# Ranking experts by token count and running them in strips of 128, 64 or 32 slots

## The chip, the cores and the metric

One Trainium2 chip, one of its cores. The metric is device time of one execution in microseconds (us), the median of several runs. TensorE (PE) has two clock levels, 1.2 and 2.4 GHz; the profile gives the granted share of the higher one. All times here come from one profiled execution, its trace, or the three timed runs.

## The reference

Two networks follow each other on a sequence of 256 tokens, width 1024. The first has two layers, each an attention and spatial-gating mixer, then a mixture of experts (MoE). The second is an attention block with an MLP and a recurrent (rwkv) block with an MLP, beside a context stream of its own. The change is in the MoE:

```python
# per layer, T = 256 tokens, D = 1024, 64 experts, top 8 of them for each token
scores = sigmoid(xt @ router_w)
eidx   = top_k(masked(scores + router_bias), 8)     # 4 of 8 groups of experts survive first
wts    = scores[eidx] / sum(scores[eidx]) * 2.5
routed = sum over the 8 experts e of a token:  wts[e] * ((silu(x @ w_gate[e]) * (x @ w_up[e])) @ w_down[e])
out    = routed + (silu(xt @ ws_gate) * (xt @ ws_up)) @ ws_down
```

`w_gate[e]` and `w_up[e]` are 1024 x 256, `w_down[e]` is 256 x 1024, all float32: 3.15 MB for an expert, 201.3 MB for a layer. 256 x 8 = 2048 pairs of a token and an expert fall on 64 experts, 32 on the average. With the inputs of the reference the fullest experts of layer 0 get 109, 99, 73, 56, 55 tokens, those of layer 1 get 75, 73, 71, 67, 63; from the 33rd on by rank no expert has more than 27 and 30.

## The kernel before

`moe` runs twice. It computes the router (lines 507 to 556), gives every pair of token and expert its place in the expert's list (`pos`, 558 to 568), and works in **groups of 256 slots**. A group is 4 experts with 64 slots each; an expert with more than 64 tokens sends the rest to a "wild" block of 64 slots. There are 16 groups of fixed experts and one of 4 wild blocks, 17 in all. Should there be more wild blocks than 4, `overflow` runs a loop; with the inputs here there are 3 and 4.

A group is two **pairs**, each of 128 slots, so that two experts fill the 128 partitions of a PSUM tile. Its steps, all on PE through `mm` (line 75):

- `pick`: a one-hot matrix `oh` (VectorE) gathers the tokens of the 256 slots, 32 products of 128 x 256 into `gat`; ScalarE and VectorE move them to `xe`.
- `up`: for each pair, 8 slices of the width times 2 experts, products with 64 columns of `xe` as weights and 512 columns of gate and up weights streaming, into `gu`. An expert uses one half of the array's columns. Each product in float32 is two records in the trace.
- `down`: silu and product (`hs`, `hm`), two transposes (`hp`), then products with `w_down` into `yps`; ScalarE and VectorE scale by the slot's weight `wsl` and split the result into `yH` and `yL`.
- `scatter`: 16 products with the transposed one-hot `ohT` into `sca`; VectorE adds them to the result.

Expert weights are fetched by SP (`fetch`, line 625) into tiles of 1 MB from a pool of 7 (`we`): 2 tiles for gate and up of an expert (two DMAs of 512 KB each), 1 for down. The address is a constant. The wild blocks' weights are gathered by POOL with an index (`wild_weights`).

Between the groups the second network's context stream runs as **side work**: `side_work(BG_GROUP / 2)` is called twice in a group and emits steps until their nominal cost (the number that each yields) is 7.25 us, so 14.5 a group. In layer 0 it is attention and an MLP, with weights of their own, in layer 1 the rwkv context. The rest of it runs later beside the second network (`late_path`).

The framework's scheduler sets the final order on each engine. PE and SP then run in that order: a PE instruction that waits for weights holds all behind it, and an SP transfer that waits for a free tile holds all transfers behind it.

Of the kernel before, what the change touches and what calls it, by code (L numbers as in the profile page):

```python
# [13 lines left out]
F32 = mybir.dt.float32  # L14
F32R = mybir.dt.float32r
I32 = mybir.dt.int32
# [11 lines left out]
NWILD = 4  # L28
NBLK = NE + NWILD
SLOT = 64  # L30
MAXOVER = 32
WU = 2048
WP = 1024
BG_MIX = 4
BG_GROUP = 14.5
# [6 lines left out]
class Net:  # L42
# [55 lines left out]
    def wtile(self, shape, srcs, name="w"):  # L98
        v = self.wbuf(shape, name)
        for sl, src in srcs:  # L100
            self.nc.sync.dma_start(v if sl is None else v[(slice(None),) + sl], src)
        return v

    def setup(self):
# [10 lines left out]
        self.identR = c.tile([P, P], F32R, name="identR")  # L115
        nc.vector.tensor_copy(self.identR, self.ident)
        self.ios = c.tile([P, SLOT], F32, name="ios")
        nc.gpsimd.iota(self.ios, pattern=[[1, SLOT]], base=0, channel_multiplier=0,
# [10 lines left out]
        self.slotp = c.tile([P, 1], F32, name="slotp")  # L129
        nc.vector.tensor_copy(self.slotp[:64], pf[:64])  # L130
        nc.vector.tensor_scalar_add(self.slotp[64:], pf[64:], -64.0)
        names = ["c", "c_2", "c_ctx_2"]
        st = c.tile([24, P], F32, name="cst0")
# [5 lines left out]
        nc.scalar.activation(cc, ps, AF.Silu)  # L139
        self.lhs1 = c.tile([P, KT, 32], F32, name="lhs1")  # L140
# [360 lines left out]
    def moe(self, l, x, row, mc, mce, rw, rb):  # L501
# [44 lines left out]
        mask = pp.tile([P, 2, NE], F32, name="mask")  # L546
        nc.vector.tensor_scalar(mask, mr, 3.0e38, None, op0=OP.is_equal)
        self.wt = mp.tile([P, 2, NBLK], F32, name="wt")
        wt = self.wt[:, :, :NE]
        nc.vector.tensor_tensor(wt, sc, mask, op=OP.mult)  # L550
        wsum = pp.tile([P, 2], F32, name="wsum")
        nc.vector.reduce_sum(wsum, wt, axis=AX.X)
        wrec = pp.tile([P, 2], F32, name="wrec")
        nc.vector.reciprocal(wrec, wsum)
        for t in range(2):
            nc.vector.tensor_scalar(wt[:, t, :], wt[:, t, :], wrec[:, t:t + 1], 2.5, op0=OP.mult, op1=OP.mult)
# [5 lines left out]
        cn = self.tr([NE, P], "cn")  # L562
        for t in range(2):
            self.mm(cn, mask[:, t, :], self.ones, t == 0, t == 1)
        self.pos = mp.tile([P, 2, NBLK], F32, name="pos")
        pm = self.pos[:, :, :NE]
        nc.vector.scalar_tensor_tensor(pm, rk, 1000.0, mask, op0=OP.add, op1=OP.mult)
        nc.vector.tensor_scalar_add(pm, pm, -1000.0)
        nb = pp.tile([NE, P], F32, name="nb")
        nb1 = pp.tile([NE, P], F32, name="nb1")  # L570
        nc.vector.tensor_scalar(nb, cn, 64.0, None, op0=OP.is_gt)
        for th in (128.0, 192.0):
            nc.vector.tensor_scalar(nb1, cn, th, None, op0=OP.is_gt)
            nc.vector.tensor_tensor(nb, nb, nb1, op=OP.add)
# [7 lines left out]
                                       op0=OP.mult, op1=OP.add)  # L582
        nover = mp.tile([1, 1], I32, name="nover")
        nc.vector.tensor_copy(nover, self.se[0:1, 1, NE - 1:NE])
        idx = mp.tile([P, NWILD], I32, name="idx")
        self.wild(l, self.iow[:, 0:NWILD], NWILD, self.pos[:, :, NE:], self.wt[:, :, NE:], idx, pp)

# [29 lines left out]
        with tc.If(rv > NWILD):  # L617
            self.overflow(l, mce)
# [3 lines left out]
        posT, wHL = self.tables(self.pos, self.wt, NBLK, mp)  # L622
        nq = NBLK // 4

        def fetch(q, pr):
            if q == NE // 4:
                return self.wild_weights(l, [idx[:, 2 * pr + u:2 * pr + u + 1] for u in range(2)])
            b = 4 * q + 2 * pr
            gus = [[self.wtile([2, 4, 256], [((v,), dap(i[n], (l * NE + b + u) * D * 256 + 1024 * a,
                                                        [[KT * 256, P], [256, 4], [1, 256]]))  # L630
                                             for v, n in enumerate(("w_gate", "w_up"))], "gu")
                    for u in range(2)] for a in range(2)]
# [90 lines left out]
    def pick(self, pos, b0, wHL, mce, wk):  # L723
# [36 lines left out]
        for h in range(2):  # L760
            nc.vector.reduce_sum(wsl[64 * h:64 * h + 64, :], wps[64 * h:64 * h + 64, :, h, :], axis=AX.X)
# [1091 lines left out]
```

## Time and profile before

| | us |
|---|---|
| median of 3 runs (lowest, highest) | 3387.86 (3383.33, 3391.14) |
| the profiled execution | 3384.59 |
| its span | 3382.8 |
| mean granted clock | 0.928 |

| engine | busy us | share of the span |
|---|---|---|
| PE | 3123.4 | 92% |
| VectorE (DVE) | 1866.9 | 55% |
| ScalarE (ACT) | 1244.5 | 37% |
| POOL | 484.9 | 14% |

The two MoE layers' groups fill 331 to 1165 us and 1471 to 2222 us, 1585 us together. PE is busy there nearly all the time, and the 16 DMA engines for 0.87 and 0.83 of it. Matmuls are pipelined, so a record is longer than the step from one to the next; rates are read from starts.

### The profile page before, as it was taken

What the parts mean: (1) busy time and instruction counts of PE and PEld (TensorE: products, weight loads), DVE (VectorE), ACT (ScalarE), POOL (GpSimd) and SP (SyncE); (2) the same over time, 40 slices, a digit from 0 to 9 for tenths busy, and PEclk for the clock granted to TensorE, in tenths of its full rate; (3) what the DMA queues carried; (4) which work ended last, traced back from release to release, by engine and by line L of the source; (5) the groups of instructions that cost most, each with busy time, mean ns of one, the idle gap of its engine ahead of it and who ended that gap; (6) DMA issues with size and microseconds to landing.
All of it is one profiled execution on the core that took longest, in us unless ns stands there. A gap on an engine that the chain in (4) does not pass through costs nothing.

```text
span 3382.8 us, 51453 instructions
## 1 busy us (share of the span) xinstructions
PE 3123.4 (92%) x20494; PEld 2095.9 (62%) x20494; DVE 1866.9 (55%) x3553; ACT 1244.5 (37%) x2170; POOL 484.9 (14%) x675
## 2 busy tenths in 40 slices
PE   6998999999999999999999999879999897889899
PEld 2776444554555687765455455556588786777698
DVE  3666444333344675753354345487777757475477
ACT  2563334232223356421232232245444453332343
POOL 1111000000000100110000100213023205243022
PEclk9999999999999999999999999979999895566799
DMA  9764987989988876478888887634425440001352
GB/s 346 276 220 147 374 321 297 349 343 348 336 306 314 307 249 231 173 276 297 331 317 312 332 329 297 254 111 164 151 93 170 132 131 7 10 8 63 146 187 88
DMA packets 240852, 773.33 MB, mean 229 GB/s; under 512 B 24672, under 2 KB 39944, under 8 KB 208864
## 3 DMA queue, kind: packets, MB, share of 16 engines
q1 hardware_dynamic: 230896, 728.56, 59.0%
q0 software_dynamic: 9376, 40.35, 3.3%
q8 instruction: 165, 2.70, 0.3%
q10 hardware_dynamic: 336, 1.06, 0.1%
q14 instruction: 79, 0.65, 0.1%
HBM read 763.73 MB, written 6.18 MB: 228 GB/s over the span
## 4 chain that ended last, share of the span: by engine, by line
PE 43%; DVE 9%; ACT 2%; issue 1%; DMA 0%; POOL 0%; DVEq 0%; SPq 0%; ACTq 0%; POOLq 0%
PE gu L75 7%; PE mu L75 5%; PE w L75 4%; PE yps L75 3%; PE rk L75 2%; PE zy L75 2%; PE gat L75 2%; PE sca L75 2%; PE rv L75 1%; PE rsc L75 1%; PE r L75 1%; PE sa L75 1%; PE aq L75 1%; DVE wl L232 1%; DVE MT L1488 1%
## 5 line engine op out<-in xcount | busy, mean ns | idle before, releaser
L232 DVE TENSOR_TENSOR wl<-w,wh 128x1024 fp32r<-128x1024 f32 (+1 forms) x432 | 467.2, 1087 | 295.1 <-ACT wh L231 289.6
L231 ACT CAST wh<-w 128x1024 fp32r<-128x1024 f32 (+1 forms) x432 | 378.3, 882 | 490.3 <-PE mu L75 135.8
L75 PE MATMUL gu<-gu,xe 128*64 128x512 f32 x2048 | 535.5, 600 | 0.2 <-DMA gu<-in_w_up_dram 0.2
L75 PEld LDWEIGHTS gu<-gu,xe 128*64 128x64 f32 x2048 | 154.2, 137 | 272.4 <-issue 254.8
L75 PE MATMUL yps<-dn,hTe 128*64 128x512 f32 x1024 | 269.8, 611 | 2.4 <-ACT hTe L797 1.6
L807 DVE SCALAR_TENSOR_TENSOR yL<-yps,wsl,yH 128x512 fp32r<-128x512 f32 x136 | 101.7, 750 | 222.4 <-ACT yH L806 222.0
L75 PE MATMUL mu<-hTH,wh 128*128 128x256 f32 x768 | 218.8, 289 | 2.9 <-ACT wh L231 1.6
L75 PE MATMUL mu<-hTL,wh 128*128 128x256 f32 x768 | 217.0, 286 | 0.0
L75 PE MATMUL mu<-hTH,wl 128*128 128x256 f32 x768 | 210.4, 288 | 1.9 <-DVE wl L232 1.9
L784 DVE TENSOR_TENSOR hm<-hs,gu 128x256 f32<-128x256 f32 x68 | 41.5, 610 | 255.8 <-ACT hs L782 255.8
L806 ACT ACTIVATE yH<-yps,wsl 128x512 fp32r<-128x512 f32 x136 | 93.5, 688 | 220.2 <-PE yps L75 213.8
L75 PEld LDWEIGHTS yps<-dn,hTe 128*64 128x64 f32 x1024 | 85.7, 139 | 135.3 <-issue 123.9
L75 PEld LDWEIGHTS mu<-hTH,wh 128*128 128x128 f32 x768 | 149.1, 194 | 12.8 <-issue 4.9
L75 PE MATMUL w<-wl,aTH 128*128 128x512 f32 x384 | 152.8, 398 | 4.4 <-DVE wl L232 4.3
L75 PEld LDWEIGHTS mu<-hTL,wh 128*128 128x128 f32 x768 | 148.9, 194 | 4.0 <-issue 2.5
L75 PE MATMUL w<-wh,aTL 128*128 128x512 f32 x384 | 150.6, 393 | 0.5 <-DVE aTL L232 0.5
L75 PEld LDWEIGHTS mu<-hTH,wl 128*128 128x128 f32 x768 | 144.4, 194 | 10.4 <-issue 4.8
L75 PEld LDWEIGHTS gat<-oh,xL 128*128 128x128 f32 x544 | 103.5, 190 | 75.9 <-issue 57.9
L782 ACT ACTIVATE hs<-gu 128x256 f32<-128x256 f32 x68 | 26.1, 383 | 331.2 <-PE gu L75 330.9
L75 PE MATMUL adaps<-adaw,lhs 128*32 128x512 f32 x768 | 122.9, 653 | 26.5 <-DMA adaw<-in_w_ada_dram 20.5
L75 PE MATMUL gat<-oh,xL 128*128 128x256 f32 x544 | 144.7, 301 | 1.1 <-DVE oh L729 1.1
L75 PE MATMUL w<-wh,aTH 128*128 128x512 f32 x384 | 138.3, 398 | 4.1 <-DVE y L1114 2.6
(601 smaller groups left out, 6669.5 us busy)
## 6 DMA issues: line engine op xcount, KB each, us to landing
gu<-in_w_gate_dram SPq DMA_DIRECT2D x256, 512.0 KB
gu<-in_w_up_dram SPq DMA_DIRECT2D x256, 512.0 KB
dn<-in_w_down_dram SPq DMA_DIRECT2D x128, 1024.0 KB
w<-in_mlp_w_dram SPq DMA_DIRECT2D x96, 1024.0 KB
adaw<-in_w_ada_dram SPq DMA_DIRECT2D x48, 1024.0 KB
adaw<-in_ada_w_dram SPq DMA_DIRECT2D x48, 1024.0 KB
w<-in_w_in_dram SPq DMA_DIRECT2D x30, 1024.0 KB
w<-in_rwkv_w_rkv_dram SPq DMA_DIRECT2D x20, 1024.0 KB
```

Source lines behind the costliest of these rows:

```text
L75: return self.nc.tensor.matmul(out, lhsT, rhs, start=start, stop=stop, skip_group_check=True)
L231: self.nc.scalar.copy(h, f)
L232: self.nc.vector.tensor_tensor(l, f, h, op=OP.subtract)
L782: nc.scalar.activation(hs, gu[:, :256], AF.Silu)
L784: nc.vector.tensor_tensor(hm.rearrange("q j p -> q p j"), hs.rearrange("q (p j) -> q p j", j=2), gu[:, 256:].rearrange("q (p j) -> q p j", ...
L806: nc.scalar.activation(yH[:, sl], y, AF.Copy, scale=g["wsl"][:, p_:p_ + 1])
L807: nc.vector.scalar_tensor_tensor(yL[:, sl], y, g["wsl"][:, p_:p_ + 1], yH[:, sl], op0=OP.mult, op1=OP.subtract)
L1488: nc.vector.transpose(T[r, :, c].rearrange("s n t -> s t n"), FA[p, w].rearrange("n s t -> n t s"))
```

## The change

The 64 experts are ranked on chip by their token count. The 4 fullest get 128 slots each, the next 28 get 64, the last 32 get 32. That is 2 groups of two 128-slot experts, 7 of four 64-slot experts and 4 of eight 32-slot experts: 13 groups of 256 slots, in the order given by `ORDER`. The wild group is gone; `overflow` would run if any expert had more tokens than its slots, which the counts above do not reach. Weights are fetched by rank, so the addresses come from a list of experts `ei` that SP reads into registers. The side work of a group depends on its strip: 0, 12 or 40 us nominal, 244 for a layer against 246.5.

```diff
+CAPS = ((4, 128), (28, 64), (32, 32))
+GROUP = 256
+ORDER = (128, 64, 32, 64, 64, 32, 64, 32, 64, 64, 32, 64, 128)
-BG_GROUP = 14.5
+BG_GROUP = {128: 0, 64: 12, 32: 40}
...
+        cn = self.tr([P, P + NE], "cn")
+        for h in range(2):
+            for t in range(2):
+                self.mm(cn[64 * h:64 * h + 64, :P], mask[:, t, :], self.ones, t == 0, t == 1)
+        for t in range(2):
+            self.mm(cn[:, P:], self.ones, mask[:, t, :], t == 0, t == 1)
...
+        nc.vector.scalar_tensor_tensor(kc, cn[:, 0:1], 64.0, self.slotp[64], op0=OP.mult, op1=OP.subtract)
+        nc.vector.scalar_tensor_tensor(kr, cn[:, P:], 64.0, self.ioe, op0=OP.mult, op1=OP.subtract)
+        nc.vector.tensor_scalar(kr, kr, kc, None, op0=OP.is_gt)
+        nc.vector.reduce_sum(rank, kr, axis=AX.X)
+        for h in range(2):
+            r = slice(64 * h, 64 * h + 64)
+            nc.vector.tensor_scalar(pm2[r, h], self.ioe[r], rank[r], None, op0=OP.is_equal)
+        self.mm(eps, ebc, pm2[:NE, 0], True, True)
+        nc.vector.tensor_copy(self.ei, eps[0:1])
...
+        for t in range(2):
+            self.transpose(mps[:, t, :], mw[:, t].rearrange("p a b -> p (a b)"))
+        nc.scalar.copy(mwT, mps)
+        for t in range(2):
+            self.mm(mso[:, t].rearrange("p a b -> p (a b)"), mwT[:, t, :], pm2.rearrange("p a b -> p (a b)"), True, True)
+        nc.vector.tensor_copy(mask, mso[:, :, 0])
+        nc.scalar.copy(self.wt, mso[:, :, 1])
...
-        self.wild(l, self.iow[:, 0:NWILD], NWILD, self.pos[:, :, NE:], self.wt[:, :, NE:], idx, pp)
...
-        with tc.If(rv > NWILD):
+        with tc.If(rv > 0):
             self.overflow(l, mce)
...
+            r0, w = groups[q]
+            k = P // w
+            with tc.issue_after(behind.pop(0)) if len(behind) > 1 else ExitStack():
+                rvs = [nc.values_load(self.ei[0:1, r0 + pr * k + u:r0 + pr * k + u + 1],
+                                      engines=[mybir.EngineType.SP], min_val=0, max_val=NE - 1) for u in range(k)]
+            src = lambda n, u, j: i[n][l, bass.DynSlice(rvs[u], 1)].rearrange("e (p j) f -> p (e j) f", j=j)
...
         for j in range(KT):
             for v in range(2 if wild else 1):
-                for u in range(2):
+                for u in range(k):
...
-                        self.mm(gu[64 * u:64 * u + 64, :].rearrange("p (a b) -> p a b", a=2), sx(j, u),
+                        self.mm(gu[w * u:w * u + w, :].rearrange("p (a b) -> p a b", a=2), sx(j, u),
                                 gus[j // 4][u][:, :, j % 4, :], j == 0, j == KT - 1)
...
-                for u in range(2):
-                    self.mm(y[64 * u:64 * u + 64, :], hT[:, j, 64 * u:64 * u + 64], dn[u][:, j, sl], j == 0, j == 1)
+                for u in range(P // w):
+                    self.mm(y[w * u:w * u + w, :], hT[:, j, w * u:w * u + w], dn[u][:, j, sl], j == 0, j == 1)
```

The bytes of a transfer and its rows of 4 KB stay as they are. Three places of the built programs show what moves.

SP, fetching expert weights in layer 0 (`gu` tiles are gate and up, `dn` is down). Before:

```order
L101 DMA gu_2805<-in_w_gate_dram 128x1024
L101 DMA gu_2805<-in_w_up_dram 128x1024
L101 DMA dn_2808<-in_w_down_dram 128x2048
L101 DMA dn_2810<-in_w_down_dram 128x2048
L101 DMA gu_2841<-in_w_gate_dram 128x1024
L101 DMA gu_2841<-in_w_up_dram 128x1024
```

After, at the first 32-slot group:

```order
L102 ISA
L102 DMA gu_3440<-in_w_gate_dram 128x1024
L102 ISA
L102 DMA gu_3440<-in_w_up_dram 128x1024
L689 TENSOR_LOAD ei_2428
L689 ISA x2
```

An address computation stands ahead of every transfer, and each fetch is preceded, two fetches early, by one register load for each expert (three more follow the one shown).

PE, the first 64-slot group that is in its stride, layer 0 (`adaps`, `asps`, `atp` are side work). Before:

```order
L75 MATMUL gu<-gu,xe 64x512 x9
L75 MATMUL adaps<-adaw,lhs_100 32x512 x4
L75 MATMUL asps<-kT,qT 128x256
L75 MATMUL adaps<-adaw,lhs_100 32x512 x4
L75 MATMUL asps<-kT,qT 128x256
L75 MATMUL gu<-gu,xe 64x512 x7
L79 MATMUL atp<-ident,ap 128x128 x4
L79 MATMUL hp<-ident,hm 128x128 x2
L75 MATMUL asps<-kT,qT 128x256 x2
L75 MATMUL gu<-gu,xe 64x512
L75 MATMUL yps<-dn,hTe 64x512 x8
```

After, the first 32-slot group:

```order
L76 MATMUL gu<-gu,xe 32x512 x17
L80 MATMUL atp<-ident,ap 128x128 x4
L76 MATMUL asps<-kT,qT 128x256 x2
L80 MATMUL atp<-ident,ap 128x128 x4
L76 MATMUL aops<-apT,v 64x256 x4
L76 MATMUL adaps<-adaw,lhs_117 32x512 x8
L76 MATMUL gu<-gu,xe 32x512
L76 MATMUL asps<-kT,qT 128x256
L76 MATMUL gu<-gu,xe 32x512
L76 MATMUL asps<-kT,qT 128x256
L76 MATMUL gu<-gu,xe 32x512 x13
```

A pair's products come in runs of 16 instead of 8, each of which needs four 1 MB tiles at once instead of two, with more side work between the runs.

PE, from the router's last use to the shared expert (`shp`, `shd`), layer 0. Before:

```order
L75 MATMUL shp<-hT,w 128x256 x22
L75 MATMUL rk<-mask,triS 128x64
L75 MATMUL rk<-mask,ones 128x64
L75 MATMUL rk<-mask,triS 128x64
L75 MATMUL cn<-ones,mask 64x128 x2
L75 MATMUL shp<-hT,w 128x256 x4
L79 MATMUL aps<-ident,araw 128x128 x4
L75 MATMUL adaps<-adaw,lhs_100 32x512 x8
L75 MATMUL sps<-triS,nb 128x64
L75 MATMUL sps<-triI,nb 128x64
L75 MATMUL shd<-w,sT 128x512 x8
```

After:

```order
L76 MATMUL shp<-hT,w 128x256 x22
L76 MATMUL cn<-ones,mw 64x128 x4
L76 MATMUL cn<-mw,ones 128x64 x2
L76 MATMUL shp<-hT,w 128x256 x4
L80 MATMUL aps<-ident,araw 128x128 x4
L76 MATMUL adaps<-adaw,lhs_117 32x512 x8
L76 MATMUL eps<-pm_2408,ebc 128x64
L80 MATMUL mps<-ident,mw 128x128 x2
L76 MATMUL shd<-w,sT 128x512 x8
L76 MATMUL mso<-pm_2408,mwT 128x128 x2
L76 MATMUL aq<-wh,hoH 128x512 x2
```

The count of blocks (`cn`, then `sps`) that the branch to `overflow` needs came ahead of `shd`; now the ranking does, and the products `rk`, `cs` and `sps` come after it, between 42 products of side work (`aq`).

## Rows read from the trace of the kernel before

**Rows 1.** Windows by stage: length, busy time (instructions) by engine, clock, DMA share, GB/s

```profile
331.00:1165.00 834.00, 803.78 (x3963) 424.54 (x3962) 353.36 (x709) 258.78 (x506) 39.65 (x54) 0.99 0.87 328
1165.00:1425.00 260.00, 251.89 (x1653) 201.58 (x1651) 170.54 (x283) 135.88 (x209) 19.88 (x21) 0.99 0.68 237
1471.00:2222.00 751.00, 721.23 (x4493) 387.01 (x4494) 326.80 (x644) 200.21 (x365) 63.38 (x123) 0.98 0.83 309
```

**Rows 2.** Waits in 331 to 1165: us in total, times, longest; SP's, then PE's

```profile
SPq L101 <- PE gu L75: 230.0, 63, 10.9
SPq L101 <- PE yps L75: 182.5, 36, 13.2
...
PE hp L79 <- DVE hm L784: 8.8, 11, 1.2
```

**Rows 3.** PE by shape, 331 to 1165: xcount, busy us, mean ns, idle before

```profile
L75 PE MATMUL gu<-gu,xe 128*64 128x512 f32 x1024 | 271.0, 602 | 0.0
L75 PE MATMUL yps<-dn,hTe 128*64 128x512 f32 x512 | 143.1, 610 | 0.8 <-ACT hTe L797 0.3
```

**Rows 4.** Timeline of PE: start us, length, records, idle before them

```profile
393.20 4.50 PE L75 MATMUL gu<-gu,xe 128*64 128x512 f32 x18
397.64 1.06 PE L75 MATMUL adaps<-adaw,lhs 128*32 128x512 f32 x8
398.64 0.70 PE L75 MATMUL asps<-kT,qT 64*128 64x256 f32 x2
...
412.39 3.35 PE L75 MATMUL yps<-dn,hTe 128*64 128x512 f32 x12
415.68 0.38 PE L75 MATMUL gat<-oh,xL 128*128 128x256 f32 x1
```

**Rows 5.** The same, single gathers and scatters, and the shared expert's full-width products

```profile
324.11 7.13 PE L75 MATMUL shd<-w,sT 128*128 128x512 f32 x16
...
392.65 0.40 PE L75 MATMUL sca<-yH,ohT 128*128 128x512 f32 x1
392.89 0.39 PE L75 MATMUL sca<-yL,ohT 128*128 128x512 f32 x1
...
416.13 0.28 PE L75 MATMUL gat<-oh,xH 128*128 128x256 f32 x1
416.24 0.28 PE L75 MATMUL gat<-oh,xL 128*128 128x256 f32 x1
```

**Rows 6.** One window of 20 us with the DMA engines full, columns as in rows 1

```profile
360.00:380.00 20.00, 19.57 (x104) 9.02 (x101) 9.80 (x27) 11.40 (x24) 3.23 (x5) 1.00 1.02 413
```

**Rows 7.** The page, 40 slices of 84.6 us: GB/s

```profile
GB/s 346 276 220 147 374 321 297 349 343 348 336 306 314 307 249 231 173 276 297 331 317 312 332 329 297 254 111 164 151 93 170 132 131 7 10 8 63 146 187 88
```

**Rows 8.** Windows of 20 us with PE idle for part, columns as in rows 1

```profile
280.00:300.00 20.00, 8.29 (x36) 6.64 (x36) 17.67 (x30) 7.60 (x12) 5.26 (x4) 0.75 0.74 249
500.00:520.00 20.00, 15.43 (x66) 6.42 (x63) 6.30 (x27) 7.42 (x19) 0.00 (x0) 0.83 0.64 225
```

**Rows 9.** Line 616 and tile gu on SP: ns min/median/max, first and last start

```profile
L616 SPq TENSOR_LOAD <-nover x2: 449/462/474, 325.0 to 1463.1; - x2
L616 SPq FUSED_REGOPS  x2: 164/172/181, 325.5 to 1463.6; - x2
...
L101 SPq DMA_DIRECT2D gu<-in_w_gate_dram x256: 327/328/2410, 331.3 to 2128.3; - x128
```

**Rows 10.** Timeline, from the router's mask to the first expert weights, layer 0

```profile
313.26 0.23 DVE L547 TENSOR_SCALAR mask<-mr 128x128 f32<-128x128 f32 x1
...
324.79 0.13 DVE L584 CAST nover<-se 1x1 int32<-1x1 f32 x1
...
331.27 0.34 SPq L101 DMA_DIRECT2D gu<-in_w_gate_dram  x1
```

**Rows 11.** Timeline, the wild group of layer 1

```profile
2172.96 1.02 POOL L702 DMA_INDIRECT wgu<-in_w_gate_dram,idx  x1 [0.16 <-issue]
...
2183.35 1.04 PE L75 MATMUL gu<-wgu,xe 128*64 128x256 f32 x4
```

More of the change, by code (lines that the diff above doesn't have):

```diff
@@ L100, in wtile @@
         for sl, src in srcs:
-            self.nc.sync.dma_start(v if sl is None else v[(slice(None),) + sl], src)
+            self.load = self.nc.sync.dma_start(v if sl is None else v[(slice(None),) + sl], src)
         return v
@@ new lines, in moe @@
+        nc.vector.tensor_copy(ebc, self.pf[:NE].to_broadcast([NE, P]))
+        capc = pp.tile([NE, 1], F32, name="capc")
+        capr = pp.tile([P, NE], F32, name="capr")
+        for e in range(len(CAPS), 0, -1):
+            n = sum(v[0] for v in CAPS[:e])
+            nc.gpsimd.memset(capc[:n], float(CAPS[e - 1][1]))
+            nc.gpsimd.memset(capr[:, :n], float(CAPS[e - 1][1]))
+        pm2 = pp.tile([P, 2, NE], F32, name="pm2")
+        nc.gpsimd.memset(pm2, 0.0)
+        cn = self.tr([P, P + NE], "cn")
@@ L551, in moe @@
+        self.eid = mp.tile([P, NE], F32, name="eid")
+        nc.scalar.copy(self.eid, eps)
+        nc.vector.tensor_tensor(wu, sc, mask, op=OP.mult)
         wsum = pp.tile([P, 2], F32, name="wsum")
-        nc.vector.reduce_sum(wsum, wt, axis=AX.X)
+        nc.vector.reduce_sum(wsum, wu, axis=AX.X)
         wrec = pp.tile([P, 2], F32, name="wrec")
@@ L561, in moe @@
         self.mm(rk[:, 1, :], self.triS, mask[:, 1, :], False, True)
[L562 to L566, printed above, removed]
+        self.pos = pm = mp.tile([P, 2, NE], F32, name="pos")
         nc.vector.scalar_tensor_tensor(pm, rk, 1000.0, mask, op0=OP.add, op1=OP.mult)
         nc.vector.tensor_scalar_add(pm, pm, -1000.0)
+        cs = self.tr([NE, P], "cs")
+        for t in range(2):
+            self.mm(cs, mask[:, t, :], self.ones, t == 0, t == 1)
         nb = pp.tile([NE, P], F32, name="nb")
         nb1 = pp.tile([NE, P], F32, name="nb1")
[L571 to L574, printed above, removed]
+        for n, th in enumerate((0.0, 64.0, 128.0, 192.0)):
+            o = nb1 if n else nb
+            nc.vector.tensor_scalar(o, cs, capc, th, op0=OP.subtract, op1=OP.is_gt)
+            if n:
+                nc.vector.tensor_tensor(nb, nb, nb1, op=OP.add)
         sps = self.tr([P, 2, NE], "sps")
@@ L621, in moe @@
         wk = wks.enter_context(self.pool(name=f"mwk{l}", bufs=2))
[L622 to L630 removed]
+        posT, wHL = self.tables(self.pos, self.wt, NE, mp)
@@ L635, in fetch, with start @@
+            behind.append(self.load.ins)
             return gus, dn, False
-        start = lambda q: self.pick(self.pos[:, :, 4 * q:4 * q + 4], 4 * q, wHL[:, :, 4 * q:4 * q + 4, :], mce, wk)
+        behind = []
+        def start(q):
+            r0, w = groups[q]
+            sl = slice(r0, r0 + GROUP // w)
+            return self.pick(self.pos[:, :, sl], r0, wHL[:, :, sl, :], mce, wk, w)
         g = drain_last(start(0))
         for q in range(nq):
+            bg = BG_GROUP[groups[q][1]]
```

113 lines of the change are left out of this document (69 added, 44 removed).

## The prediction

> **What bounds the kernel now.** I read the windows by stage first. In both MoE layers PE is busy for 96% of the stretch (803.8 of 834 us, 721.2 of 751), the DMA engines for 0.87 and 0.83 of it [rows 1]. The second network has neither MoE nor expert weights, so the change acts on 834 + 751 = 1585 us. Busy PE alone does not tell who waits for whom, so the waits come next: in layer 0 SP waits 230 and 182.5 us for PE to free weight tiles, and the largest entry in PE's own list is 8.8 us, for VectorE; an expert's weights are not in that list at all [rows 2]. So **PE sets the pace of the groups**, and the DMA engines have 13% to 17% to spare. That spare share is what the change lives on.
>
> **The price of a group on PE.** I take steps from start to start, since a record (602 ns) is longer than the step [rows 3]. A run of 18 `gu` records goes from 393.20 to 397.64, 0.247 us a record; 12 records of `yps` go from 412.39 to 415.68, 0.274 [rows 4]. I take 0.25 for both. Gathers step by 0.115, scatters by 0.235 [rows 5]. A group of four 64-slot experts has 2 pairs x 32 `gu` records (1024 records in 16 groups, [rows 3]), 32 of `yps`, 32 gathers, 16 scatters, and some ten small products at up to 0.25:
> 16.0 + 8.0 + 3.7 + 3.8 + 2.5 = 34 us.
> Seventeen are 578 us. Of layer 0's 834 us, 256 are left for 246.5 nominal us of side work and PE's idle time; of layer 1's 751 us, 173 are left.
>
> **Fewer groups.** Thirteen in place of 17 take 4 x 34 = 136 us of PE from each layer. The two 128-slot groups have full-width products: 16 records of the shared expert take (7.13 - 0.59)/15 = 0.436 us each [rows 5]; 32 + 16 of them are 21 us instead of 24, so 31 a group, and another 6 us go. PE then needs 11 x 34 + 2 x 31 = 436 us for the groups of a layer.
>
> **Strips of 32.** A 32-slot group has 128 + 64 = 192 records, each 32 columns wide. Their nearest row is `adaps`, whose 32-column products also stream 512 columns: 8 records from 397.64 to 398.64, 0.125 us each [rows 4]. That is 24 us, as for strips of 64. Bounds: 0.109 if four strips share one full-width product perfectly (21 us), 0.25 if only two overlap (48 us). I take the row.
> The Trainium skill, TensorEngine Tiling (Array Packing), Theoretical Speedup, says that strips of 32 can give up to four times the throughput. By it a group's 192 records would take 192 x 0.436/4 = 21 us, 3 us less than by the row, and eight such groups at most 24 us less in the sum.
>
> **Side work.** 244 nominal us replace 246.5, so it costs about what it did: 254 and 171 us. Where it stands matters: 0 in the 128-slot groups, 12 in the 64-slot, 40 in the 32-slot. In layer 0 a nominal us is 1.04 real ones, in layer 1 0.70. PE's need by group is then, in layer 0: 31, 34 + 12.5 = 46.5, 34 + 41.5 = 75.5; in layer 1: 31, 42.4, 62. The sums, 690 and 607, would be the new lengths if weights were always there. The order also ends the side work a little earlier, before the last group; what the boundary of a stage gains by it, the next stage gives back.
>
> **Bytes.** They become the second bound. Layer 0 moves 0.328 x 834 = 273.6 MB, layer 1 0.309 x 751 = 232 MB [rows 1]. The wild gathers, 4 x 3.15 = 12.6 MB, go; 201.3 MB of expert weights stay; so the side work carries 59.7 and 18 MB. A 32-slot group fetches 8 x 3.15 = 25.2 MB, and its side work brings 9.7 in layer 0 and 2.9 in layer 1: **34.9 and 28.1 MB**. A 64-slot group needs 15.5 and 13.5 MB, a 128-slot group 6.3. At a full rate of 0.40 MB/us (413 GB/s in a window whose share is 1.02, [rows 6]) the 32-slot groups take 87 and 70 us, more than PE's 75.5 and 62; the others (39, 34 and 16 us) stay below PE.
>
> The pool doesn't cover that: a run of 16 products wants four tiles at once, of seven, so three are fetched ahead, 3 MB, against a deficit of (87 - 75.5) x 0.40 = 4.6 MB in layer 0. **So 32-slot groups go at the pace of the weights, the rest at PE's.** Which rate? The single full window is the upper end, 0.40; the rate that the stages had, 0.328 and 0.309, the lower. I take the best 84.6 us slice of the page, 374 GB/s [rows 7], because it is as long as such a group and lies at the start of the first MoE, where SP finds free tiles: 34.9/0.374 = 93.3 and 28.1/0.374 = 75 us.
>
> Layer 0: 4 x 93.3 + 7 x 46.5 + 2 x 31 = 761, against 834: -73.
> Layer 1: 4 x 75 + 7 x 42.4 + 2 x 31 = 659, against 751: -92.
>
> **Edits on SP.** 64 register loads a layer at 0.46 + 0.17 + 0.03 us, and 320 address computations at 0.17 [rows 9], are 42 and 54 us on a queue that issues a 512 KB transfer in 0.33. Four tiles of `gu` then take 8 x 0.5 = 4 us to issue and 10.5 to move: hidden behind the transfers under way. If the cover is gone (the four loads stand ahead of the next transfer) it is 32 x 0.65 = 21 us a layer, in the 32-slot groups. I take 0; the range takes both.
>
> **Router.** The ranking adds some ten dependent small steps between the mask (313.26) and the block count (324.79) on which all engines branch [rows 10], and PE's order puts `shd` (7.13 us, [rows 5]) and 42 side products at 0.235 = 10 us ahead of the branch. They are work that is done anyway, so PE isn't idle; the weights start late. The first transfer came at 331.27, when `shd` was done; I put it at about 342. The first group now needs one tile, not two, so of 11 us I charge 5 a layer (0 to 11).
>
> **The end.** In layer 1 the wild group's second pair was gathered by POOL from 2172.96, and PE could begin on it at 2183.35 [rows 11], 10.4 us in which it had only short side products. That goes: -10. The last group's own chain to the norm stays exposed, in both. Router and end cancel.
>
> **Sum.** 3384.6 - 73 - 92 + 10 - 10 = 3220 us for the profiled execution (its span and 1.8 us around it). The median of the three runs is 3.3 us above that execution, so 3223.
>
> **Rivals.**
> *The cushions hold.* If seven tiles and the lighter neighbours bridge most of the deficit, the 32-slot groups cost PE's 75.5 and 62 plus some 3 us: 702 and 619 for the layers, so 132 + 132 = 264 us off, 3124 by the median. For it: 32-slot groups never follow each other. Against it: four tiles at once.
> *The rate doesn't rise.* SP's order is fixed, and a transfer for side work that waits for its tile holds the experts' behind it. If the 32-slot groups get the 0.328 and 0.309 MB/us of before, they take 106 and 91 us; with 64-slot groups at 47.3 and 43.7 the layers are 819 and 732 long: -34, 3354. For it: the mean share of a whole MoE was never above 0.87. Against: then it was PE that held SP back [rows 2].
> *A slower clock.* Where PE idles, the granted clock falls: 0.75 of 2.4 GHz in a window with 8.3 us of PE work, 0.83 with 15.4 [rows 8]. If PE, waiting for weights in short bursts, ran the 32-slot groups at 0.75, their need would be 75.5/0.75 = 101 and 62/0.75 = 83 us, over the transfers' 93 and 75: 8 x 7.5 = 60 us, 3283.
> The Trainium skill, TensorE: Matmul & The Clock Gate, HAM oscillation, describes just this: bursts of products that are shorter than the wait for the next slice run on the slow clock every time. The trace agrees in direction, by the two windows named.
> *Slower than before.* PE and transfers take turns: a run frees its four tiles only at its end, and if the next four are then fetched with nothing ahead, each of a group's six runs costs 10.5 us of transfer, 32 x 0.125 = 4 of products, and 8.6 or 6.3 of other work. That is 139 and 125 us a group, 4 x 46 + 4 x 50 = 384 over the forecast, 3607. It decides from 165/8 = 21 us a group over my 93 and 75, that is when nearly half of the overlap is lost. Against it: three tiles are always ahead, and the side work has a pool of its own.
> *It doesn't do what it says.* Were an expert over its slots, the loop of 16 passes would run with 6.3 MB each, over 250 us a layer. The counts (109, 99, 73, 56 in 128 slots, then 55 or 63 in 64, 27 or 30 in 32) exclude it.
>
> **How the numbers follow.** Forecast 3223, with its own range of 3170 to 3290 (full windows' rate 0.40, or 0.35 with 21 us of SP's loads): 0.50. Cushions hold, 3124: 0.12. Slower clock, 3283: 0.09. Rate as before, 3354: 0.20. Turns: 0.08, of which 0.06 are slower than before and 0.01 within 0.2% (about 7 us, what a measurement of this kernel can tell from no change). 0.01 for the loop or anything else that is slower. The range of 8 in 10 runs from 3130 to 3350: it leaves out the turns and the ends of the first and fourth case. Faster 0.92, same 0.01, slower 0.07.
>
> **What would show it.** In the new profile, MoE stages of about 760 and 660 us with a DMA share of 0.9 or more; PE's waits for `gu` and `dn` transfers, absent now, of 10 to 20 us in each 32-slot group and near none in the others; a 32-column `gu` record at 0.125 us; a 64-slot group near 46 us. Wrong if 32-column records step by 0.2 or more (strips don't overlap), if PE waits for weights in 64-slot groups too, or if SP's waits for PE stay as long as they are, which would mean that PE still bounds all.

## The result, and the profile after

| | before | after |
|---|---|---|
| median of 4 runs, us | 3388.43 | 3303.30 (3290.33 to 3305.50) |
| ratio, 95% interval | 1 | 0.974 (0.972 to 0.977) |
| profiled execution, span, us | 3382.8 | 3288.6 |
| PE busy, us | 3123.4 | 2951.3 |
| mean granted clock | 0.928 | 0.912 |

The kernel is 85 us faster where 165 were forecast. 3303 lies in the range of 8 in 10 (3130 to 3350), but outside the forecast's own range (3170 to 3290).

Windows of the changed kernel by stage, answering to [rows 1] (length, busy time by engine, clock, DMA share, GB/s): first MoE, what follows it, second MoE, the rest.

```profile
346.00:1120.00 774.00, 720.14 (x3745) 391.13 (x3743) 322.30 (x636) 239.91 (x473) 25.51 (x37) 0.97 0.91 339
1120.00:1391.00 271.00, 238.97 (x1501) 184.13 (x1497) 177.14 (x304) 129.57 (x198) 30.34 (x42) 0.95 0.66 234
1443.00:2178.00 735.00, 657.57 (x4504) 337.71 (x4502) 292.63 (x591) 170.38 (x322) 54.83 (x126) 0.91 0.80 288
2178.00:3288.00 1110.00, 991.79 (x8010) 821.38 (x8010) 778.00 (x1383) 474.31 (x811) 291.96 (x374) 0.84 0.33 110
```

The first MoE is shorter, with the DMA engines at 0.91. In the second PE is busy for 64 us less than before, but the DMA share has fallen to 0.80 and the clock to 0.91. To compare like with like I cut both traces at the start of the same events: first router product (`lg`), first `gu` product, last `gy` (VectorE's step on the last scatter). "Idle" and "slow" are sums over windows of 4 us: length minus busy, and busy times (1 - granted clock).

| stretch, us | before | after | difference | idle | slow |
|---|---|---|---|---|---|
| up to the first router | 305.0 | 308.2 | +3 | 54 to 55 | 8 to 9 |
| router to first expert product, layer 0 | 36.8 | 46.9 | +10 | 1 to 3 | 0 |
| first MoE | 809.4 | 764.6 | -45 | 26 to 51 | 8 to 15 |
| to the second router | 289.7 | 270.9 | -19 | 17 to 32 | 2 to 7 |
| router to first expert product, layer 1 | 39.8 | 52.4 | +13 | 4 to 0 | 5 to 0 |
| second MoE | 733.6 | 734.0 | 0 | 20 to 76 | 8 to 52 |
| the rest | 1168.5 | 1111.6 | -57 | 138 to 120 | 158 to 140 |
| sum | 3382.8 | 3288.6 | -94 | +78 | +34 |

What is left when idle and slow time are taken off, PE's work at full clock, fell by 206 us. So 112 us of what PE saves come back as waiting and as slower products: 100 in the second MoE, 52 in the first and the stretch behind it, less 36 in the rest.

Where did the saved work go? Here each product counts from its start to the next one's, idle time taken off and at the full clock. The products of the experts' groups fall from 569 to 455 us in the first MoE and from 552 to 456 in the second. All other products, side work mostly, grow from 207 to 242 in the first MoE and fall from 271 to 232 behind it. In the second MoE they stay (152 and 149); ahead of it they grow from 26 to 48, and in the rest they fall from 872 to 848. Over the whole execution their sum is the same before and after (1803 and 1804). So side work fills part of the room, and part of the gain shows in the stretches that it left.

PE's waits in the changed kernel, 330 to 1120, then 1420 to 2185 (us in total, times, longest), answering to [rows 2]:

```profile
PE gu L76 <- DMA gu<-in_w_gate_dram: 11.1, 1, 11.1
PE gu L76 <- DMA gu<-in_w_up_dram: 8.3, 4, 4.1
```

```profile
PE gu L76 <- DMA gu<-in_w_up_dram: 24.1, 9, 7.1
PE rtk L80 <- DVE BK L1465: 15.6, 6, 3.8
PE hp L80 <- DVE hm L858: 11.9, 11, 4.7
```

PE now waits for expert weights, as forecast, but for 5 to 6 us in a 32-slot group (19.4/4, 24.1/4) and not 10 to 20. The prediction named one more sign, SP's waits for PE to free weight tiles. In the first MoE they fell, from 412 us to 279. In the second they did not. Before (1471 to 2222), then after (1443 to 2178):

```profile
SPq L101 <- PE gu L75: 276.1, 69, 16.0
SPq L101 <- PE yps L75: 160.4, 32, 10.1
```

```profile
SPq L102 <- PE gu L76: 220.8, 49, 17.9
SPq L102 <- PE yps L76: 209.2, 25, 22.0
```

436 us and 430: there PE still holds the transfers back for as long as before. Much of the loss is inside the products. PE by shape, 32-column products alone, first MoE, then second (xcount, busy us, mean ns, idle before), answering to [rows 3]:

```profile
L76 PE MATMUL gu<-gu,xe 128*32 128x512 f32 x512 | 97.5, 608 | 19.4 <-DMA gu<-in_w_gate_dram 11.1 <-DMA gu<-in_w_up_dram 8.3
...
L76 PE MATMUL yps<-dn,hTe 128*32 128x512 f32 x256 | 50.5, 672 | 0.2
```

```profile
L76 PE MATMUL gu<-gu,xe 128*32 128x512 f32 x512 | 110.9, 719 | 24.1 <-DMA gu<-in_w_up_dram 24.1
...
L76 PE MATMUL yps<-dn,hTe 128*32 128x512 f32 x256 | 56.6, 728 | 0.1
```

At 0.125 us a record, 512 would take 64 us and 256 would take 32. The timeline of PE in the third 32-slot group of layer 1 shows why they take more (start us, length, records):

```profile
1840.32 4.48 PE L76 MATMUL gu<-gu,xe 128*32 128x512 f32 x34
1844.73 0.66 PE L80 MATMUL rtk<-ident,BK 128*128 128x128 f32 x4
1845.31 1.10 PE L76 MATMUL rsc<-ZL,BK 64*128 64x64 f32 x8
1846.34 1.05 PE L76 MATMUL gu<-gu,xe 128*32 128x512 f32 x2
1847.32 1.10 PE L76 MATMUL rsc<-ZL,BK 64*128 64x64 f32 x8
1848.35 1.04 PE L76 MATMUL gu<-gu,xe 128*32 128x512 f32 x2
1849.33 0.71 PE L76 MATMUL rcum<-tri,sg 128*128 128x128 f32 x4
```

34 records in one piece take 4.41 us to the next start, 0.130 each. A piece of two records is one product of one strip, alone between side products, and takes 0.98 us, as much as four strips side by side would (8 x 0.125). Presumably the scheduler puts such a product where it reckons with its tile being there before its three neighbours' tiles; no run shows its reckoning. From start to next start, idle time taken off, a 32-column `gu` record takes 0.170 us in the first MoE and 0.198 in the second, a `yps` record 0.182 and 0.205. At the full clock it would be 0.164 to 0.171 in both layers; the rest is time at 1.2 GHz. Of `gu` products that stand alone there are 19 and 18, 0.95 to 1.05 us each at the full clock and 1.8 at the lower.

The same group, windows of 3 us (length, PE busy, clock, DMA share, GB/s):

```profile
1861.00:1864.00 3.00, 1.50 (x11) 1.00 0.95 306
1864.00:1867.00 3.00, 0.00 (x0) 0.87 1.00 410
1867.00:1870.00 3.00, 2.45 (x12) 0.50 1.07 408
1870.00:1873.00 3.00, 3.00 (x20) 0.50 0.71 264
1873.00:1876.00 3.00, 3.00 (x21) 1.00 0.16 38
...
1888.00:1891.00 3.00, 3.00 (x58) 0.50 0.05 14
```

PE waits 5 us for a tile with the DMA engines full, then works at 1.2 GHz (0.50) until 1873, and by then the DMA engines run dry (0.71, then 0.16). The Trainium skill, TensorE: Matmul & The Clock Gate, HAM oscillation, describes bursts that each begin on the slow clock after a wait; these windows agree. Of the three (lone products, waits, clock) the experiments below take the first apart; waits and clock they don't separate.

### The profile page after: what moved, and what is told of

It reads as the page before. It is cut to its first block, busy times and chain, and to the rows that moved or that the text cites. A ratio compares the mean times of both kernels' runs of the same rounds, so it can differ in the third digit from the quotient of the medians.

```text
span 3288.6 us, 51224 instructions
## 1 busy us (share of the span) xinstructions
PE 2951.3 (90%) x19750; PEld 1984.6 (60%) x19750; DVE 1782.4 (54%) x3388; ACT 1178.4 (36%) x2066; POOL 456.2 (14%) x665
## 4 chain that ended last, share of the span: by engine, by line
PE 40%; DVE 10%; ACT 3%; DMA 2%; issue 2%; POOL 0%; SPq 0%; DVEq 0%; ACTq 0%; POOLq 0%
PE gu L76 7%; PE mu L76 6%; PE w L76 4%; PE yps L76 3%; PE zy L76 2%; PE gat L76 2%; PE rsc L76 2%; PE rk L76 1%; PE rv L76 1%; PE sca L76 1%; PE r L76 1%; PE sa L76 1%; DVE wl L240 1%; DVE MT L1563 1%; DVE N L1550 1%
## 5 line engine op out<-in xcount | busy, mean ns | idle before, releaser
L76 PE MATMUL gu<-gu,xe 128*32 128x512 f32 (+2 forms) x2048 | 501.2, 632 | 44.7 <-DMA gu<-in_w_up_dram 32.4
L76 PEld LDWEIGHTS gu<-gu,xe 128*32 128x32 f32 (+2 forms) x2048 | 134.9, 131 | 279.7 <-issue 235.0
L76 PE MATMUL yps<-dn,hTe 128*32 128x512 f32 (+2 forms) x1024 | 259.7, 662 | 3.4 <-ACT hTe L872 2.7
L882 DVE SCALAR_TENSOR_TENSOR yL<-yps,wsl,yH 128x512 fp32r<-128x512 f32 x104 | 77.9, 750 | 184.2 <-ACT yH L881 183.9
L76 PEld LDWEIGHTS yps<-dn,hTe 128*32 128x32 f32 (+2 forms) x1024 | 74.1, 135 | 135.7 <-issue 124.2
L858 DVE TENSOR_TENSOR hm<-hs,gu 128x256 f32<-128x256 f32 x52 | 31.6, 608 | 218.7 <-ACT hs L856 218.6
L881 ACT ACTIVATE yH<-yps,wsl 128x512 fp32r<-128x512 f32 x104 | 71.4, 687 | 202.2 <-PE yps L76 193.1
L1074 POOL TENSOR_TENSOR x<-x,opt 128x512 f32<-128x512 f32 x56 | 98.7, 1784 | 258.6 <-DVE opt L1073 258.6
L818 DVE TENSOR_SCALAR xe<-gat,mce 128x256 f32<-128x256 f32 x104 | 56.3, 542 | 107.6 <-ACT xe L816 106.9
L76 PEld LDWEIGHTS gat<-oh,xL 128*128 128x128 f32 x416 | 79.7, 192 | 55.8 <-issue 44.5
```

The source lines that it names most:

```text
L76: return self.nc.tensor.matmul(out, lhsT, rhs, start=start, stop=stop, skip_group_check=True)
L818: nc.vector.tensor_scalar(xe[:, 1, :], ps[:, 1, :], mce[:, 1, 2 * jj + 1:2 * jj + 2], mce[:, 0, 2 * jj + 1:2 * jj + 2], op0=OP.mult, op1=O ...
L858: nc.vector.tensor_tensor(hm.rearrange("q j p -> q p j"), hs.rearrange("q (p j) -> q p j", j=2), gu[:, 256:].rearrange("q (p j) -> q p j", ...
L881: nc.scalar.activation(yH[:, sl], y, AF.Copy, scale=g["wsl"][:, p_:p_ + 1])
L882: nc.vector.scalar_tensor_tensor(yL[:, sl], y, g["wsl"][:, p_:p_ + 1], yH[:, sl], op0=OP.mult, op1=OP.subtract)
L1074: (self.nc.vector if last else self.nc.gpsimd).tensor_tensor(x[:, t, sl], x[:, t, sl], tt, op=OP.add)
```

## Experiments

Ratios are to the kernel before, run on the same chip. The changed kernel is at 0.974, 3303 us.

**Half tiles.** In the MoE the pool is 14 tiles of 512 KB, not 7 of 1 MB; the tiles of the shared expert and of `overflow` are halved likewise.

```diff
-            with net.weights(f"we{l}", 7):
+            with net.weights(f"we{l}", 14):
...
-            gus = [[self.wtile([2, 4, 256], [((v,), src(n, u, KT)[:, 4 * a:4 * a + 4, :])
+            gus = [[self.wtile([2, 2, 256], [((v,), src(n, u, KT)[:, 2 * a:2 * a + 2, :])
...
-                    for u in range(k)] for a in range(2)]
+                    for u in range(k)] for a in range(4)]
```

> In the MoE phases the weight pool has 14 tiles of 512 KB in place of 7 of 1 MB, and each tile is loaded and released by itself: a four-strip run wants 2 MB of tiles at once instead of 4 MB, so 5 MB can be on the way while it runs, instead of 3. Theory TURNS (what is missing in the 32-slot groups is lost because the DMA engines stand still once three tiles are ahead, and PE once fewer than four are there): the 32-slot groups of layer 1 fall from some 90 us to 80 or less, those of layer 0 from 91 to 87, 3235 to 3270 us in all. Theory SIDE CHAINS (the 40 us of side work in a 32-slot group run at the pace of their own chain through VectorE): within 10 us of 3303. Theory SP (the queue that issues the transfers is the limit): twice as many transfers, slower than 3303 by 20 us or more.

3318 us, 0.981 (0.977 to 0.985). Against TURNS as I wrote it. PE's idle time in the two MoE layers did fall (51 and 76 to 46 and 47 us), but the unbroken pieces of 32-column `gu` products grew from 58 to 78 in the first MoE and from 51 to 65 in the second, their records take 0.19 us in both, and side work slid out behind both layers: the stretches after them are 23 and 38 us longer. More, smaller tiles invite more lone products. SP's part isn't separated by this run.

**Constant addresses.**

```diff
-                rvs = [nc.values_load(self.ei[0:1, r0 + pr * k + u:r0 + pr * k + u + 1], ...
-            src = lambda n, u, j: i[n][l, bass.DynSlice(rvs[u], 1)].rearrange("e (p j) f -> p (e j) f", j=j)
+            b = r0 + pr * k
+            src = lambda n, u, j: i[n][l, b + u:b + u + 1].rearrange("e (p j) f -> p (e j) f", j=j)
```

> The ranks are still worked out, but the weights are fetched at constant addresses in the order of the expert numbers, so the result is not the reference's: no register loads, no address computations on SP, and the first weights need not wait for the ranking. Theory SP: the 64 loads and their waits cost in the groups, so the groups get shorter and the whole gains 40 us or more. Theory TURNS and theory SIDE CHAINS: the groups keep their lengths; only the start of each MoE comes earlier, by 10 to 15 us a layer, 3270 to 3285.

3301 us, 0.976 (0.972 to 0.979): nothing. SP's loads and address computations are hidden. Nor does the start come earlier (first expert product at 354.6 and 1440.2 us, 355.1 and 1443.0 with ranks): PE's own order, with `shd` and side products ahead, sets it.

**No strips of 32.**

```diff
-CAPS = ((4, 128), (28, 64), (32, 32))
+CAPS = ((4, 128), (60, 64))
-ORDER = (128, 64, 32, 64, 64, 32, 64, 32, 64, 64, 32, 64, 128)
+ORDER = (128,) + 15 * (64,) + (128,)
-BG_GROUP = {128: 0, 64: 12, 32: 40}
+BG_GROUP = {128: 0, 64: 16.3}
```

> Ranking and two 128-slot groups stay, but all other experts get 64 slots: 17 groups a layer, side work 16.3 a 64-slot group, none in the 128-slot groups. If the whole gain comes from having 13 groups instead of 17: 3380 to 3400 us. If about half of it comes from elsewhere, namely from side work that stands earlier so that less of it trails behind the second MoE (the stretch after the last MoE product was 57 us shorter): 3330 to 3350, with that stretch still some 50 us shorter than before.

3386 us, 0.999 (0.998 to 1.001). Ranking and the 128-slot groups pay for themselves and no more; the gain hangs on the 32-slot strips. But it doesn't stand in the stretches where these run: the first MoE takes 766 us without them and 765 with them, the second 725 and 734. Expert products fall there from 552 to 455 us and from 546 to 456, but other products (191 to 242, 143 to 149) and idle and slow time (24 to 66, 36 to 128) fill the room. What gets shorter are the stretches behind, 293 to 271 and 1202 to 1112 us.

**Half of the 32-slot strips.**

```diff
+CAPS = ((4, 128), (44, 64), (16, 32))
+ORDER = (128,) + 4 * (64,) + (32,) + 3 * (64,) + (32,) + 4 * (64,) + (128,)
+BG_GROUP = {128: 0, 64: 15, 32: 40}
```

> 16 of the 64 experts in 32-slot strips instead of 32, 44 in 64-slot strips: 15 groups a layer, of which two have eight experts. Half of the step from 17 groups (3386) to 13 (3303) in a straight line is 3345. If the DMA engines' spare time is what runs out (each eight-expert group takes more bytes than fit under its own products, but neighbours have room): the first two groups gain more than the last two, 3300 to 3325. If each lone product costs the same wherever it stands: 3345 within 10.

3343 us, 0.987 (0.984 to 0.989): the straight line, in the sum. The expert products in the two MoEs fall evenly (1098, 1003, 911 us with none, two and four such groups a layer), and idle and slow time of the whole grow no faster at the end (482, 530, 559), so nothing points to the layer's spare DMA time running out. By stretch there is no line (first MoE 766, 755, 765 us, second 725, 736, 734), since side work moves between them.

**Side work elsewhere.**

```diff
-BG_GROUP = {128: 0, 64: 12, 32: 40}
+BG_GROUP = {128: 20, 64: 29, 32: 0}
```

> Side work 20 in a 128-slot group, 29 in a 64-slot group, none in a 32-slot group (243 a layer as before). Theory SIDE CHAINS: a 32-slot group without side work falls from 90 us to what its 25.2 MB take, 63 to 67 us, and a 64-slot group grows to some 55 us in layer 1 and 64 in layer 0: layer 1 gains 20 us, layer 0 loses 50, 3320 to 3345 in all. Theory TURNS: without side work nothing fills the waits either, a 32-slot group stays at 80 us or more, and the whole is slower than 3370.

3297 us, 0.974 (0.971 to 0.978). Both theories miss, because the run tests neither: SP's 1016 transfers stand in the same order as in the changed kernel, PE's products nearly so (126 of 19750 places differ), and the groups begin within ten microseconds of where they did. The scheduler has put side work back to where it was, whatever the table asks for in a group; of these two tables only the layer's sum counted.

**No side work in layer 1.**

```diff
-            bg = BG_GROUP[groups[q][1]]
+            bg = BG_GROUP[groups[q][1]] * (1 - l)
```

> No side work is asked for in the second MoE; all that it did there comes after it. By the terms of the forecast the stage is then 4 x 67 (25.2 MB at 0.374) + 7 x 34 + 62 = 570 us from its first to its last product instead of 734. Theory CHAIN (the 128 us in which PE idles or runs at the lower clock there come from the side work's own chain): idle and slow time fall under 50 us, 560 to 590. Theory TURNS (they come from four tiles at once out of seven): they stay at 80 us or more, 600 to 660. The whole is slower than 3303 in either case, since what trails is not covered: 3340 to 3420.

One run, 3564 us. The second MoE takes 596 us. Its PE waits (us in total, times, longest):

```profile
PE gu L76 <- DMA gu<-in_w_up_dram: 91.2, 30, 10.4
PE hp L80 <- DVE hm L858: 23.2, 20, 1.4
```

CHAIN fails by its own sign: without any side work idle and slow time are 154 us, not under 50. Where the 128 us came from with side work the run doesn't show, since without it PE has less to do beside the same transfers. From a group's first `gu` product to the next group's, a 32-slot group takes 71 us there (mean of four) and the 64-slot group behind it 37; 71 is near the forecast's pace of weights (25.2 MB at 0.374, 67 us). The total I had wrong by far. What is moved costs 138 us inside the second MoE (734 - 596) and 449 behind it (1561 - 1112), where nothing covers its own chains.

**Whole runs.** In a 32-slot group the product that reads the last tile leads its run, and the rest is queued behind it. With the first pair's four `dn` tiles held, three of seven would be left for the second pair, so the first pair's `down` comes ahead of the second `up`. The same was done in `down` for each half of the width.

```diff
+WHOLE = (32,)
...
+            for a in range(2):
+                first = part(4 * a, k - 1)
+                with self.tc.issue_after(first.ins):
+                    for j in range(4 * a, 4 * a + 4):
+                        for u in range(k):
+                            if (j, u) != (4 * a, k - 1):
+                                part(j, u)
...
+            if groups[q][1] == 32:
+                self.down(g, 0, *h[0], w[0][1], wk)
             w.append(fetch(q, 1))
```

> In 32-slot groups alone: the product that reads the tile loaded last stands first in each run of 16 (gate and up) and of 8 (down), and the others of the run are queued behind it, so the planner cannot put a strip's product by itself earlier; the first pair's down products come ahead of the second pair's up products in the code, so that seven tiles are enough. Theory PIECES (a product of one strip that stands alone takes PE as long as four side by side; in the changed kernel the 32-column records take 0.16 to 0.19 us each in place of 0.125): the records come to 0.13 to 0.14 us each, some 65 us of PE go, 3235 to 3260 in all. Theory FILL (the lone products stand where PE would wait for the fourth tile in any case): PE's waits for gu transfers grow by about what the products save, 3290 to 3315.

3250 us, 0.958 (0.956 to 0.961). PIECES. The 32-column rows of the first MoE:

```profile
L77 PE MATMUL gu<-gu,xe 128*32 128x512 f32 x512 | 64.4, 643 | 17.6 <-DMA gu<-in_w_up_dram 17.6
...
L77 PE MATMUL yps<-dn,hTe 128*32 128x512 f32 x256 | 32.3, 649 | 1.4 <-DMA dn<-in_w_down_dram 1.4
```

and a run on PE's timeline:

```profile
446.98 3.64 PE L77 MATMUL gu<-gu,xe 128*32 128x512 f32 x32
450.55 0.66 PE L81 MATMUL atp<-ident,ap 128*128 128x128 f32 x4
```

32 records in 3.57 us, 0.112 each; in the mean 0.124 (`gu` and `yps`) in the first MoE, 0.145 and 0.167 in the second, where more runs fall into time at the lower clock (0.112 to 0.116 at the full one). PE's waits for `gu` transfers are 17.6 and 18.9 us in the two layers, no longer than in the changed kernel (19.4 and 24.1). Its idle time in all grew by 20 us in the first MoE (51 to 72) and not in the second (76 to 76). So lone products had filled some waiting, but little. Not all of the saving shows, though: at the full clock the products of the experts' groups fell by 89 us, and in the whole execution idle time grew by 22 and slow time by 38. The move of `down` by itself wasn't run.

**Whole runs in 64-slot groups too.**

```diff
-WHOLE = (32,)
+WHOLE = (32, 64)
```

> As whole_runs, and in the 64-slot groups too, where two products of one run want two tiles. PIECES: a further 0 to 15 us, since only some twenty of the 64-slot records stand alone in pairs (0.23 to 0.25 us each in the mean, as forecast). FILL: the same as whole_runs, or slower by up to 15, since PE may no longer begin a run with one tile.

**3231 us, 0.952 (0.949 to 0.955)**, better than both kernels, by 19 us more and not 0 to 15. The 64-column `gu` records go from 0.248 us in the changed kernel to 0.221 in the first MoE. The MoE layers:

```profile
355.00:1066.00 711.00, 646.17 (x3557) 365.40 (x3556) 306.23 (x607) 230.08 (x455) 22.11 (x33) 0.94 0.94 360
...
1403.00:2088.00 685.00, 596.81 (x4323) 329.28 (x4322) 289.39 (x581) 171.15 (x313) 48.71 (x114) 0.90 0.85 313
```

**The kernel before with whole runs.** The same edit to `up` and `down` of its 64-slot pairs.

```diff
+            for a in range(2):
+                first = part(4 * a, 1)
+                with self.tc.issue_after(first.ins):
...
+            first = part(0, 1)
+            with self.tc.issue_after(first.ins):
+                for j, u in ((0, 0), (1, 0), (1, 1)):
+                    part(j, u)
```

> The kernel before, with its up and down products of 64-slot pairs kept in whole runs in the same way as in whole_runs_64. If whole runs help wherever strips are used: the 64-column records there step by 0.24 in the mean, with 26 lone pairs of records a layer at 0.8 us each, so some 15 us a layer can go, 3360 to 3375 against 3388. If they help only where four tiles have to meet: within 8 us of 3388, and what whole_runs_64 gained is the change's own.

3364 us, 0.992 (0.989 to 0.995). Lone strips cost the kernel before some 28 us as well. With whole runs on both sides the change is worth 0.9519/0.9917 = 0.960, 133 us; as written it kept 85.

**Less side work in layer 1.**

```diff
-            bg = BG_GROUP[groups[q][1]]
+            bg = BG_GROUP[groups[q][1]] * (1 - 0.10 * l)
```

> The changed kernel with 0.9 times the side work in the second MoE: its order then does two of the four chunks of the context's scan features ahead of the last scatter, as the kernel before does, in place of three, and nothing else is edited. Theory BOUNDARY: the stretch behind the last MoE product grows from 1112 us by 35 to 60, to what the kernel before has (1168), the second MoE falls from 734 by 20 to 40, 3310 to 3335 in all; then the 57 us were the chunk, and the second MoE itself gained what the same chunk hid. If the stretch does not hang on the chunk: it stays within 15 us of 1112, and the whole falls by 10 us or more, since the second MoE has less to do.

3333 us, 0.982 (0.980 to 0.984). BOUNDARY: the second MoE falls by 23 us to 711, the rest grows by 65 to 1176. (The rwkv context is worked off in four chunks of 256 features.) Other products than the experts' fall by 26 us in the second MoE and grow by 33 in the rest, where idle and slow time grow by 34 as well. So a chunk that lies beside expert products costs a third of what it costs behind them, and 25 to 30 us of the change's 85 (0.982 against 0.974) are this chunk's place. The forecast took that at nothing. The rest is graded by that chunk in the other kernels too: 1112 us where all of it is done before the last scatter; 1140 to 1149 (half_tiles, whole_runs, whole_runs_64, fewer_32) where its scores (`rsc`) are done but its inverse is not or not all; 1168 to 1202 (the kernel before, less_side, before_whole, no_32) where half of the scores are done at most. The size is not exact, since SP's order in the rest differs as well.

**More side work in layer 1**, in the kernel before and in the whole-run version.

```diff
-            self.side_work(BG_GROUP / 2)
+            self.side_work(BG_GROUP * (1 + 0.4 * l) / 2)
```

> The kernel before, with 1.4 times the side work asked for in the second MoE: its order then does three of the four chunks of the context's scan features ahead of the last scatter, as the changed kernel's does, in place of two. Theory BOUNDARY (a part of the changed kernel's gain is that this chunk lies beside expert products instead of behind them: the stretch after the last MoE product was 57 us shorter, the second MoE no shorter): that stretch falls by 40 to 60 us, the second MoE grows by 20 to 40, 3355 to 3380 in all. If what is moved is only paid for in another place, as the forecast took it: within 8 us of 3388.

> whole_runs_64 with 1.4 times the side work in the second MoE (three chunks of the context's scan features ahead of the last scatter; whole_runs_64 has two). BOUNDARY: PE idles 88 us in the second MoE there and 130 after it, so the chunk fits where it stands now: 3190 to 3220. If what is moved is only paid for in another place: within 10 us of 3231.

3451 us, 1.019 (1.015 to 1.023), and 3290 us, 0.972 (0.968 to 0.976): 56 and some 60 us slower than without the edit, against BOUNDARY on its face. The second MoE grew by 39 and 21 us, as expected; but the rest grew too, by 24 and 32. SP's waits behind the last MoE product, kernel before with more side work:

```profile
SPq L101 <- PE adaps L75: 145.8, 10, 128.4
```

and PE's windows there (length, busy, clock, DMA share, GB/s):

```profile
2340.00:2380.00 40.00, 15.89 (x333) 0.50 0.00 1
2380.00:2420.00 40.00, 31.77 (x359) 0.50 0.00 1
```

One transfer of `adaw` waits 128 us for its tile (110 in the other kernel; 14 and 16 without the edit), and the weights of the next network's attention stand behind it on SP's queue. The `aq` products end 198 and 183 us after the MoE in place of 86 and 74. In the rest other products fell by 28 and 27 us, as the chunk left it, but idle and slow time grew by 52 and 58. The long hold is the likely cause, though no run removes it alone; so these two runs don't tell what the place of a chunk is worth.

## Why the prediction was right or wrong

- **What bounds, sign and mechanism.** Right for the kernel before and in sign: PE set the pace, there is no gain without the 32-slot strips (no_32: 0.999), and PE came to wait for weights only in their groups. Wrong on where the time goes: the stretches with these groups are no shorter than without them (765 against 766, 734 against 725 us), and the gain shows behind them, where side work left.
- **The 64-slot records at 0.25.** Right: 0.248 (`gu`) and 0.271 (`yps`) in the first MoE, 0.240 and 0.270 in the second.
- **Strips of 32 at 0.125.** Right for a whole run (0.112 to 0.130), wrong for the kernel: 0.170 to 0.205 in the mean. 768 records a layer cost 134 and 154 us (512 x 0.170 + 256 x 0.182; 512 x 0.198 + 256 x 0.205), 38 and 58 more than 96. Of that some 30 a layer would be there at the full clock, too; the rest, 8 and 25, is the lower clock. (0.205 touches the prediction's sign of being wrong, 0.2, but strips do overlap.) I took the price of a record from eight that stood together, and my second listing of PE's new order already showed `gu` products by themselves, x1, between side products. This is the first step that failed. The Trainium skill, TensorEngine Tiling (Array Packing), Theoretical Speedup, gives up to four times for strips of 32: whole runs agree (0.436/0.112 = 3.9), lone products get nothing of it.
- **Bytes.** The number came out in layer 0, partly by luck. A 32-slot and the 64-slot group behind it took 140 us in the mean of four, 139.8 forecast. But in the 32-slot group's 88.6 us expert products took 43, not 34, and side work 33, not 41.5; the two errors offset each other, and 12 us were idle. In layer 1 they took 130, 117.4 forecast, which over four groups is 50 us. There the second step failed, that 32-slot groups go at the pace of the weights. The group took 84.6 us and not 75, though it moved only 23.5 MB (0.278 MB/us) and not 28.1. PE idled for 14 us of it, about as forecast (75 - 62 = 13); expert products took 49 us, not 34 (time at the lower clock included), and side work 22, not 28. So its excess is lone products and the lower clock, and SP waited for PE as long as before (430 us, 436). The 64-slot groups of that layer took 27 us and the 128-slot groups 10 more than forecast. Slow time was 52 us against 8 before; that waits set it off is what one window shows (1861 to 1876), not a run that removes them. With whole runs the pair still takes 118 us.
- **The lengths of the stages.** First MoE: 761 forecast, 765 measured. But I set it against 834, the window of [rows 1], which holds some 10 us ahead of the first product and 15 behind the last step; between the same events the stage before had 809. So -73 should have been -48, and -92 some -75, by my own numbers. An error of frame, 42 us.
- **Side work by group.** The step from 0, 12 and 40 us to a need of 31, 46.5 and 75.5 us has no ground: the scheduler doesn't keep to the table (bare_32). Nor did side work cost what it did: of the 256 us left in layer 0 only 207 were other products, the rest idle and slow time and the window's ends, and after the change they were 242.
- **Boundary at nothing.** Wrong. -57 us in the rest and -19 ahead of the second router, where other products fell by 39 us as the first MoE took in 35 more. The changed kernel does a third chunk of the context's scan ahead of the last scatter; less_side gives it back and loses 25 to 30 us.
- **SP at nothing.** Right (static_addr). **Router at +5:** the first expert product came 10 and 13 us later, but PE idled for 3 and 0 us of that, so it isn't a loss of that size. **The end at -10** was not tested by itself.
- **Rivals.** "Slower clock" (3283) came nearest in size, but in the wrong place: 34 us in all, of which 43 in the second MoE and a gain in the rest. "The rate doesn't rise" was half true: 0.328 to 0.339 in layer 0, 0.309 to 0.288 in layer 1. "Turns" had the right object, four tiles out of seven, but not the effect: PE didn't stand until four were there, it began with one strip, at the price of four.

The sum, by stretch, measured less forecast: first MoE -45 against -73 (+28), second MoE 0 against -92 (+92), routers +23 against +10 (+13), other stretches -73 (3 - 19 - 57) against -10 for the end (-63): +70 together, which is 165 less 94 of the profiled executions to within a microsecond. Open: why the second MoE, with whole runs in all groups, still takes 685 us against the 659; PE idles 88 us in it, in waits for `gu` and `dn` transfers and for VectorE's steps of the scan, and loses 55 to the lower clock.

## What to carry to other kernels

Products on strips of the array are cheap only when the strips' products stand together: look in the built order for strip products by themselves, price those at the full width, and tie a run to its last tile if the scheduler splits it. Measure a stage before and after between the same two events, or its head and tail are counted as gain. Work that is moved beside a busy engine is not given back later at the same price; look which queue it is put on, since one held transfer there can take more than the move gives. And where a scheduler can move such work, a stage's length alone doesn't show what a change in it is worth: split PE's time by what it worked on.

## What the runs showed of the hardware

- A 32-column product in float32 (512 columns streaming) takes 0.95 to 1.05 us by itself and 0.22 us (2 x 0.112) in a run of four strips, at the full clock. Full width takes 0.87 (2 x 0.436).
- In 5 us without a product (1862.6 to 1867.6) the granted clock fell to 0.50; it stayed there until 1873, and 32-column records stepped by 0.21 us in place of 0.112.
- 128 register loads and the address computations on SP cost no measurable time while the DMA engines were busy for 0.80 to 0.91 of the stage.
